# Smaller pieces for the last two weight groups of a streamed bilinear form

## The chip, the cores and the metric

The kernel runs on one core of a Trainium2 chip. The metric is the device time of one execution, in microseconds (us). The kernel before takes 88.63 us, the median of three runs (88.56 to 88.67). A profile is one recorded execution; its span, from the first to the last instruction, is 87.1 us in an execution that took 88.9 us. Times inside the profile are counted from the start of the span.

A core has several engines that run side by side: TensorE does matrix products (PE in the profile, with PEld for the loading of its stationary operand), VectorE is DVE, ScalarE is ACT, GpSimd is POOL and SyncE is SP. Data comes from the chip's memory through 16 DMA engines, which all transfers share.

## The reference

```python
batch, dim_i, dim_j, dim_k = 32, 256, 256, 128
# x: (32, 256), y: (32, 256), weight: (128, 256, 256), all float32
def reference(x, y, weight):
    return np.einsum('bi,bj,kij->bk', x, y, weight).astype(np.float32)
```

Every output element is x[b] · weight[k] · y[b]. The weight has 128 x 256 x 256 float32 values, which is 33.55 MB, and each is needed once. Reading it is the large part of the work.

## The kernel before

The 128 matrices weight[k] are treated in G = 32 groups of KK = 4. One group is laid out on 128 partitions, which hold 32 blocks of i for each of the 4 values of k, and within a partition there are IC = 8 rows of J = 256 values. A group is loaded by one DMA from the GpSimd queue, which turns float32 into bfloat16 on the way: 1 MB is read and 512 KB are written. The first group comes through another queue as float32.

```python
    w_v = weight.rearrange("(kk g) (ip ic) j -> g ip kk (ic j)", kk=KK, ic=IC)
    # ... x, y and group 0 are loaded ...
    def split(g):
        return [(0, 4), (4, 6), (6, 8)] if g == G - 1 else [(0, IC)]

    w_tiles = {}

    def load(g):
        for lo, hi in split(g):
            wt = wpool.tile([P, (hi - lo) * J], bf16, name=f"w{g}_{lo}")
            nc.gpsimd.dma_start(out=wt, in_=w_v[g][:, :, lo * J:hi * J])
            for ic in range(lo, hi):
                w_tiles[g, ic] = wt[:, (ic - lo) * J:(ic - lo + 1) * J]

    load(1)
    # ... an identity matrix is made ...
    for g in range(2, G):
        load(g)
    # ... xblk (x, one block per ic, masked per kk) and y4 are prepared ...
```

Every tile of the pool is a buffer of its own, so no load waits for a buffer. The loads share eight completion semaphores in turn, and for this reason a load is issued only when the load eight places before it has landed.

A group is then eight matmuls, one for each ic, that add up in one bank of PSUM, followed by one VectorE instruction that multiplies with y and sums over j:

```python
    for g in range(G):
        ps = pso.tile([P, J], f32)
        for ic in range(IC):
            nc.tensor.matmul(
                out=ps,
                lhsT=xblk[:, ic, :, :].rearrange("p b kk -> p (b kk)"),
                rhs=w_tiles[g, ic],
                start=(ic == 0), stop=(ic == IC - 1),
            )
        tmp = tmps.tile([P, J], f32)
        nc.vector.tensor_tensor_reduce(
            out=tmp, in0=ps, in1=y4, scale=1.0, scalar=0.0,
            op0=mult, op1=add, accum_out=acc[:, g:g + 1],
        )

    out_v = out.rearrange("b (kk g) -> b kk g", kk=KK)
    nc.sync.dma_start(out=out_v, in_=acc)
```

A matmul can start when the tile that holds its rows has landed as a whole. The last group (g = 31) comes in three pieces, of four, two and two rows; each other group comes in one piece.

Of the kernel before, what the change touches and what calls it, by code (L numbers as in the profile page):

```python
# [1 line left out]

# [4 lines left out]


@with_exitstack
def kernel(  # L10
    ctx: ExitStack,
    tc: tile.TileContext,
    x: bass.AP,
    y: bass.AP,
    weight: bass.AP,
    out: bass.AP,
):
    nc = tc.nc
    P = 128
    f32 = mybir.dt.float32  # L20
    bf16 = mybir.dt.bfloat16
    mult = mybir.AluOpType.mult
    add = mybir.AluOpType.add

    B, I = x.shape
    _, J = y.shape
    K, _, _ = weight.shape
    KK = P // B
    IP = P // KK
    IC = I // IP  # L30
    G = K // KK
    assert KK * B == P and IP * KK == P and IC * IP == I and G * KK == K

    consts = ctx.enter_context(tc.tile_pool(name="consts", bufs=1))
    wpool = ctx.enter_context(tc.tile_pool(name="wpool", bufs=1))
    psx = ctx.enter_context(tc.tile_pool(name="psx", bufs=1, space=bass.MemoryType.PSUM))
    pso = ctx.enter_context(tc.tile_pool(name="pso", bufs=4, space=bass.MemoryType.PSUM))
    tmps = ctx.enter_context(tc.tile_pool(name="tmps", bufs=2))


    w_v = weight.rearrange("(kk g) (ip ic) j -> g ip kk (ic j)", kk=KK, ic=IC)

    x_sb = consts.tile([B, I], f32)
    nc.scalar.dma_start(out=x_sb, in_=x)
    y_sb = consts.tile([B, J], f32)
    nc.scalar.dma_start(out=y_sb, in_=y)


    w0 = consts.tile([P, IC * J], f32)
    nc.sync.dma_start(out=w0, in_=w_v[0])  # L50

    def split(g):
        return [(0, 4), (4, 6), (6, 8)] if g == G - 1 else [(0, IC)]

    w_tiles = {}

# [9 lines that stand above are left out]
    ident = consts.tile([P, P], f32)  # L66
    nc.gpsimd.memset(ident, 0.0)  # L67
    nc.gpsimd.affine_select(  # L68
        out=ident, in_=ident, compare_op=mybir.AluOpType.not_equal, fill=1.0,
        base=0, pattern=[[-1, P]], channel_multiplier=1,  # L70
    )
    for g in range(2, G):
        load(g)

    mask = consts.tile([P, KK], f32)
    nc.vector.tensor_reduce(  # L76
        out=mask, in_=ident.rearrange("p (ip kk) -> p kk ip", kk=KK),
        axis=mybir.AxisListType.X, op=add,
    )


    x_rep = consts.tile([B, IC, IP, KK], f32)
    x_cols = x_sb.rearrange("b (ip ic) -> b ic ip", ic=IC)
    for ic in range(IC):
        nc.vector.tensor_copy(  # L85
            out=x_rep[:, ic, :, :],
            in_=x_cols[:, ic, :].unsqueeze(2).to_broadcast([B, IP, KK]),
        )
    xt_ps = psx.tile([P, IC, B], f32)
    for ic in range(IC):  # L90
        nc.tensor.transpose(  # L91
            out=xt_ps[:, ic, :],
            in_=x_rep[:, ic, :, :].rearrange("b ip kk -> b (ip kk)"),
            identity=ident[:B, :B],
        )


    xblk = consts.tile([P, IC, B, KK], bf16)
    for kk in range(KK):
        nc.vector.tensor_scalar(  # L100
            out=xblk[:, :, :, kk], in0=xt_ps, scalar1=mask[:, kk:kk + 1],
            scalar2=None, op0=mult,
        )


    JH = J // P
    yt_ps = psx.tile([P, JH, B], f32)
    for jh in range(JH):
        nc.tensor.transpose(  # L109
            out=yt_ps[:, jh, :], in_=y_sb[:, jh * P:(jh + 1) * P],  # L110
            identity=ident[:B, :B],
        )
    yt4 = consts.tile([P, JH, B, KK], f32)
    nc.vector.tensor_copy(  # L114
        out=yt4, in_=yt_ps.unsqueeze(3).to_broadcast([P, JH, B, KK])
    )
    y4_ps = psx.tile([P, J], f32)
    for jh in range(JH):
        nc.tensor.transpose(  # L119
            out=y4_ps[:, jh * P:(jh + 1) * P],  # L120
            in_=yt4[:, jh, :, :].rearrange("p b kk -> p (b kk)"),
            identity=ident,
        )
    y4 = consts.tile([P, J], f32)
    nc.vector.tensor_copy(out=y4, in_=y4_ps)  # L125

    w0b = wpool.tile([P, IC * J], bf16)
    for lo, hi in ((0, IC // 2), (IC // 2, IC)):
        nc.scalar.copy(out=w0b[:, lo * J:hi * J], in_=w0[:, lo * J:hi * J])  # L129
    for ic in range(IC):  # L130
        w_tiles[0, ic] = w0b[:, ic * J:(ic + 1) * J]

    acc = consts.tile([P, G], f32)
# [19 lines that stand above are left out]
# [1 line left out]
_INS = ['x', 'y', 'weight']  # L154
_OUTS = [((32, 128), 'float32')]


# [23 lines left out]
```

## Time and profile before

| What | Value |
|---|---|
| device time, median of three runs | 88.63 us (88.56 to 88.67) |
| span of the profiled execution | 87.1 us |
| TensorE busy / weight loads busy | 54.4 us (62%) / 32.6 us (37%) |
| VectorE, GpSimd, ScalarE busy | 18.6, 18.3 and 3.3 us |
| weight loads on the GpSimd queue | 33: 30 of 512 KB, 1 of 256 KB, 2 of 128 KB (as written) |
| read from memory over the span | 33.62 MB, 386 GB/s |

The busy shares say how long an engine worked over the whole span. They do not say what sets the end: for that one reads the chain of waits, which goes back from the last instruction to what released it, and the timeline of the last microseconds. In the view of the slices, the span is cut into 40 equal parts of about 2.18 us; a digit is a share in tenths.

### The profile page before, as it was taken

The page shows a single profiled execution, that of the slowest core. Times are in us where ns is not written, and L with a number is a line of the kernel's source. Part 1 is how long each engine was busy: PE and PEld are TensorE (multiplying, and loading weights), DVE is VectorE, ACT ScalarE, POOL GpSimd, SP SyncE. Part 2 cuts the span into 40 slices and gives each one's busy share as a digit, 9 for nine tenths or more (in the row PEclk, how much of TensorE's full clock was granted, in tenths as well). Part 3 has the DMA queues.
Part 4 walks back from the last instruction along what each step waited for, and adds up shares of the span by engine and source line. Part 5 has one row for each costly group of instructions (what it writes and reads, how often), then busy time and mean ns, then how long its engine had stood idle before and what let it go on. Part 6 is the DMA issues. An engine that isn't in the chain of part 4 may idle for free.

```text
span 87.1 us, 741 instructions
## 1 busy us (share of the span) xinstructions
PE 54.4 (62%) x268; PEld 32.6 (37%) x268; DVE 18.6 (21%) x79; ACT 3.3 (4%) x3; POOL 18.3 (21%) x39
## 2 busy tenths in 40 slices
PE   0416994667777843776487773754887544974870
PEld 0415653433343432433344432332444331543630
DVE  0893123011111120111101111111011211031030
ACT  2327000000000000000000000000000000000000
POOL 5980222222111221112222222012222200000000
PEclk9999999755555696557955598589555975569659
DMA  1899999999999999999999999999999999999700
GB/s 30 277 312 209 216 216 216 213 213 213 213 214 213 211 213 218 213 216 213 213 213 213 211 216 213 211 213 216 213 218 211 213 214 211 214 214 203 127 3 8
DMA packets 5139, 17.43 MB, mean 200 GB/s; under 512 B 720, under 2 KB 1040, under 8 KB 5008
## 3 DMA queue, kind: packets, MB, share of 16 engines
q0 software_dynamic: 4752, 16.26, 93.6%
q1 hardware_dynamic: 288, 1.07, 3.5%
q10 hardware_dynamic: 96, 0.07, 0.4%
q8 instruction: 2, 0.03, 0.1%
q14 instruction: 1, 0.01, 0.0%
HBM read 33.62 MB, written 0.02 MB: 386 GB/s over the span
## 4 chain that ended last, share of the span: by engine, by line
DMA 87%; PE 4%; POOL 3%; issue 2%; DVE 0%; POOLq 0%; DVEq 0%
DMA w<-in_weight_dram 87%; PE ps L137 4%; POOL w L60 3%; DVE tmp L144 0%; POOL ident L68 0%; POOL ident L67 0%; POOLq L68 0%; POOLq L165 0%; DVEq L176 0%
## 5 line engine op out<-in xcount | busy, mean ns | idle before, releaser
L137 PE MATMUL ps<-w,xblk 128*128 128x256 bf16 x248 | 50.8, 377 | 24.2 <-DMA w<-in_weight_dram 24.2
L137 PEld LDWEIGHTS <-xblk 128*128 128x128 bf16 x256 | 31.0, 130 | 46.9 <-DMA w<-in_weight_dram 34.3
L60 POOL DMA_DIRECT2D w<-in_weight_dram x33 | 17.7, 546 | 50.6 <-DMA w<-in_weight_dram 49.8
L144 DVE CUSTOM_DVE_ANT_0 tmp<-ps,y 128x256 f32<-128x256 f32 x32 | 13.6, 425 | 62.2 <-PE ps L137 62.2
L137 PE MATMUL ps<-w0b,xblk 128*128 128x256 bf16 x8 | 2.1, 411 | 1.6 <-ACT w0b L129 1.6
L91 PE MATMUL xt_ps<-ident,x_rep 32*128 32x32 f32 x8 | 1.1, 293 | 3.0 <-POOL ident L68 3.0
L144 DVE DVE_READ_ACCUMULATOR2_ANT acc<- 128x1 f32 x32 | 2.7, 83 | 0.0
L100 DVE TENSOR_SCALAR xblk<-xt_ps,mask 128x256 bf16<-128x256 f32 x4 | 2.5, 771 | 0.1
L129 ACT CAST w0b<-w 128x1024 bf16<-128x1024 f32 x2 | 2.0, 1042 | 3.2 <-DMA w<-in_weight_dram 3.2
L91 PEld LDWEIGHTS xt_ps<-ident,x_rep 32*128 32x128 f32 x8 | 0.9, 200 | 3.0 <-POOL ident L68 3.0
L85 DVE COPY x_rep<-x_sb 32x128 f32<-32x128 f32 x8 | 1.3, 236 | 2.4 <-DMA x_sb<-in_x_dram 2.4
L129 ACT ACT_TABLE_LOAD x1 | 1.3, 1283 | 1.6 <-PEq L165 1.6
L109 PE MATMUL yt_ps<-ident,y_sb 32*128 32x32 f32 x2 | 0.4, 300 | 1.1 <-DMA y_sb<-in_y_dram 1.1
L109 PEld LDWEIGHTS yt_ps<-ident,y_sb 32*128 32x128 f32 x2 | 0.3, 199 | 1.2 <-DMA y_sb<-in_y_dram 1.2
L125 DVE COPY y<-y_ps 128x256 f32<-128x256 f32 x1 | 0.4, 425 | 1.3 <-PE y_ps L119 1.3
L119 PE MATMUL y_ps<-ident,yt 128*128 128x128 f32 x2 | 0.6, 417 | 0.0
L119 PEld LDWEIGHTS y_ps<-ident,yt 128*128 128x128 f32 x2 | 0.4, 226 | 0.1
L114 DVE COPY yt<-yt_ps 128x256 f32<-128x256 f32 x1 | 0.4, 448 | 0.0
L76 DVE TENSOR_REDUCE mask<-ident 128x4 f32<-128x128 f32 x1 | 0.4, 369 | 0.0
L68 POOL TENSOR_SCALAR_AFFINE_SELECT ident<-ident 128x128 f32<-128x128 f32 x1 | 0.3, 322 | 0.1
L67 POOL MEMSET ident<- 128x128 f32 x1 | 0.2, 224 | 0.0
L165 POOL MEMSET const-float32-0.0<- 128x1 f32 x1 | 0.1, 99 | 0.2 <-issue 0.2
(3 smaller groups left out, 0.3 us busy)
## 6 DMA issues: line engine op xcount, KB each, us to landing
w<-in_weight_dram POOLq DMA_DIRECT2D x30, 512.0 KB, 19.4
w<-in_weight_dram SPq DMA_DIRECT2D x1, 1024.0 KB, 5.3
w<-in_weight_dram POOLq DMA_DIRECT2D x1, 256.0 KB, 18.3
w<-in_weight_dram POOLq DMA_DIRECT2D x2, 128.0 KB, 15.6
x_sb<-in_x_dram ACTq DMA_DIRECT2D x1, 32.0 KB, 1.7
y_sb<-in_y_dram ACTq DMA_DIRECT2D x1, 32.0 KB, 4.0
out_dram<-acc SPq DMA_DIRECT2D x1, 16.0 KB, 1.4
```

Of the source, the lines that this page charges most:

```text
L60: nc.gpsimd.dma_start(out=wt, in_=w_v[g][:, :, lo * J:hi * J])
L76: nc.vector.tensor_reduce(out=mask, in_=ident.rearrange("p (ip kk) -> p kk ip", kk=KK), axis=mybir.AxisListType.X, op=add,)
L85: nc.vector.tensor_copy(out=x_rep[:, ic, :, :], in_=x_cols[:, ic, :].unsqueeze(2).to_broadcast([B, IP, KK]),)
L91: nc.tensor.transpose(out=xt_ps[:, ic, :], in_=x_rep[:, ic, :, :].rearrange("b ip kk -> b (ip kk)"), identity=ident[:B, :B],)
L100: nc.vector.tensor_scalar(out=xblk[:, :, :, kk], in0=xt_ps, scalar1=mask[:, kk:kk + 1], scalar2=None, op0=mult,)
L109: nc.tensor.transpose(out=yt_ps[:, jh, :], in_=y_sb[:, jh * P:(jh + 1) * P], identity=ident[:B, :B],)
L114: nc.vector.tensor_copy(out=yt4, in_=yt_ps.unsqueeze(3).to_broadcast([P, JH, B, KK]))
L119: nc.tensor.transpose(out=y4_ps[:, jh * P:(jh + 1) * P], in_=yt4[:, jh, :, :].rearrange("p b kk -> p (b kk)"), identity=ident,)
L125: nc.vector.tensor_copy(out=y4, in_=y4_ps)
L129: nc.scalar.copy(out=w0b[:, lo * J:hi * J], in_=w0[:, lo * J:hi * J])
L137: nc.tensor.matmul(out=ps, lhsT=xblk[:, ic, :, :].rearrange("p b kk -> p (b kk)"), rhs=w_tiles[g, ic], start=(ic == 0), stop=(ic == IC - 1),)
L144: nc.vector.tensor_tensor_reduce(out=tmp, in0=ps, in1=y4, scale=1.0, scalar=0.0, op0=mult, op1=add, accum_out=acc[:, g:g + 1],)
```

## The change

The last group is loaded in four pieces instead of three: its last two rows come as two pieces of one row. The group before it (g = 30) is loaded in two pieces of four rows instead of one of eight. Nothing else is edited. The purpose is to let the last matmuls start before the whole of their group has landed, so that less work is left when the last byte arrives.

```diff
     def split(g):
-        return [(0, 4), (4, 6), (6, 8)] if g == G - 1 else [(0, IC)]
+        if g == G - 1:
+            return [(0, 4), (4, 6), (6, 7), (7, 8)]
+        if g == G - 2:
+            return [(0, 4), (4, 8)]
+        return [(0, IC)]
```

There are then 35 loads on the GpSimd queue instead of 33. The number and the order of the matmuls, of the weight loads of TensorE and of the VectorE instructions do not change. The first matmul of each new piece carries a wait for that piece.

## The prediction

> **What bounds the kernel now.** I read the page first, for the chain of waits and the slices, and then the end in detail: the chain in order of time, the timeline from 70 us, the DMA issues, and two tables by window. The chain and the slices:
>
> ```profile
> DMA 87%; PE 4%; POOL 3%; issue 2%; DVE 0%; POOLq 0%; DVEq 0%
> ...
> GB/s 30 277 312 209 216 216 216 213 213 213 213 214 213 211 213 218 213 216 213 213 213 213 211 216 213 211 213 216 213 218 211 213 214 211 214 214 203 127 3 8
> ...
> q8 instruction: 2, 0.03, 0.1%
> ```
>
> The stream of weights is the bound: 87% of the chain is its transfer, and the bytes written run at a flat 213 GB/s from slice 4 to slice 36. A group of 512 KB (524,288 bytes) takes 524,288 / 213,000 = 2.46 us. The change removes no byte, so all that it can save lies behind the stream. The last steps of the chain in order of time:
>
> ```profile
> 61.29 19.52 DMA w<-in_weight_dram
> 80.81 0.05 issue
> 80.85 3.44 PE ps L137 x16
> 84.30 0.02 issue
> 84.32 0.42 DVE tmp L144
> ```
>
> The last transfer on the chain is that of g = 30, not of g = 31: it lands at 80.81, and then sixteen matmuls, two whole groups, run in one unbroken row of 3.44 us. So TensorE, and not the last piece, sets the end. The timeline gives the pace of a group:
>
> ```profile
> 70.88 1.89 PE L137 MATMUL ps<-w,xblk 128*128 128x256 bf16 x8 [1.39 <-DMA w<-in_weight_dram]
> ...
> 78.43 1.05 PE L137 MATMUL ps<-w,xblk 128*128 128x256 bf16 x8 [0.60 <-DMA w<-in_weight_dram]
> ...
> 80.85 3.43 PE L137 MATMUL ps<-w,xblk 128*128 128x256 bf16 x16 [1.37 <-DMA w<-in_weight_dram]
> ```
>
> Eight matmuls take 1.89 us at one time and 1.05 us at another. The table by window shows why (columns: window, length, busy us and count of PE, PEld, DVE, ACT, POOL, granted clock, DMA share, GB/s). I cut it where the granted clock changes:
>
> ```profile
> 70.83:74.24 3.41, 2.03 (x9) 1.15 (x10) 0.43 (x2) 0.00 (x0) 0.00 (x0) 0.50 1.06 214
> 74.24:77.65 3.41, 3.40 (x16) 1.92 (x14) 0.43 (x2) 0.00 (x0) 0.00 (x0) 0.50 1.06 213
> 77.65:81.07 3.42, 1.45 (x12) 0.91 (x11) 0.87 (x4) 0.00 (x0) 0.00 (x0) 1.00 1.07 204
> 81.07:84.48 3.41, 3.21 (x16) 1.98 (x14) 0.59 (x3) 0.00 (x0) 0.00 (x0) 0.50 0.33 54
> ```
>
> A window with 1.45 us of TensorE work is followed by half clock, one with 3.40 us by full clock. The end falls into a half-clock window. One matmul took 0.42 us at half clock and 0.27 at full (the shortest and the longest in the view of the weight tiles). In a row they then follow each other every (1.89 - 0.42) / 7 = 0.21 us at half clock and every (1.05 - 0.27) / 7 = 0.11 us at full.
>
> When do the pieces of g = 31 land? The view of the DMA issues, asked for the windows that hold one issue each, gives the times from issue to landing:
>
> ```profile
> w<-in_weight_dram POOLq DMA_DIRECT2D x1, 256.0 KB, 18.3
> ...
> w<-in_weight_dram POOLq DMA_DIRECT2D x1, 128.0 KB, 16.5
> ...
> w<-in_weight_dram POOLq DMA_DIRECT2D x1, 128.0 KB, 14.7
> ```
>
> With the issue times 63.74, 66.24 and 68.68 of the timeline of POOL they land at 82.0, 82.7 and 83.4. The timeline of the last two microseconds has the eight matmuls of g = 31 start at 82.37, so its first piece waited some 0.35 us for TensorE. Its last matmul starts at 84.30 - 0.42 = 83.9, half a microsecond after the last landing. That is the slack that the change can reach.
>
> **What the Trainium skill says.** "TensorE: Matmul & The Clock Gate", section "Part 1: The HAM clock gate", has the clock either at half or at full, set by how busy the engine was in the last window of about 3.4 us, with windows that run free of the kernel. The trace agrees: windows of 3.41 us, only 0.50 and 1.00. "DMA: Bandwidth & Descriptors", section "Why a DMA increments its semaphore by 16 and not by 1", says that a transfer counts as landed only when the last of its 16 engines has posted. The trace agrees: the DMA share falls to 0.19 in the window from 82 to 83 us, so that about three engines of sixteen are left, and the final piece lands only after them. "Runtime: NRT & Kernel Launch", section "Instruction fetch mechanics", says that instructions are themselves fetched by DMA in blocks of 16 KiB; the page's q8 line has two such packets, 0.03 MB. They are an explanation for laggards that I cannot prove here. The same DMA page, section "Specifications", wants at least 512 B for line rate. The new one-row pieces write exactly 512 B per partition (256 values of 2 bytes); no transfer of this size is in this trace.
>
> **The change part by part.**
>
> The issues. The loads go from 33 to 35. POOL spends 0.55 us on each (17.7 us / 33), so 1.1 us more, beside an idle of 50.6 us. A load is issued when the one eight places before has landed. By the old times the fifth and fourth loads before the end now go at 63.74 and 66.24, the next at 68.68, and the last two when g = 26 and g = 27 land, about 70.9 and 74.1 by their matmuls. This is over 9 us before their bytes are due. It costs nothing on the path.
>
> The stream. Each DMA engine handles 8 of the 128 partitions, so it gets 8 more packets for g = 30 and 8 more for the last pieces, and two more completion packets. What does a packet cost beyond its bytes? From 20 to 30 us there are 586 packets of which 65 are completions, at 106.3% of 16 engines: 170 us / 521 = about 0.32 us for a packet of 4 KB. From 82.6 to 82.8 us five packets of 1 KB take 15.3%: 0.49 us / 5 = 0.098 us. The line through both has 0.023 us fixed per packet. But the share is over 100%, so packets overlap: by pace, 4 KB at 213 / 16 = 13.3 GB/s per engine is 0.308 us, and the bulk of the 1 KB packets (81.0 to 81.2 us) moved 210 GB/s, almost the same rate. So the cost by pace is about 0.002 us per packet. A completion takes 0.022 us (one packet, 0.7% of 16 engines, in 83.0 to 83.2 us). The sum is 16 x 0.002 + 2 x 0.022 = 0.08 us; if nothing overlapped, 16 x 0.023 + 0.044 = 0.41 us. I take 0.1: the last piece lands at 83.5.
>
> The work of g = 30. Its first half lands half a group earlier, at 80.81 - 1.23 = 79.6. Four matmuls at full clock take 0.6 us and are over by 80.2, when TensorE used to sit idle. The second half lands at 80.85; two matmuls at full clock and two at half end by 81.7. This frees TensorE about 0.7 us sooner than the 82.4 of before.
>
> The work of g = 31. TensorE now waits for its first piece, which lands at 82.05 and starts at 82.1. Eight matmuls in a row at half clock: the last starts at 82.1 + 7 x 0.21 = 83.57, if its piece is there. Piece (6, 7) is needed at 83.36 and should land near 83.15; piece (7, 8) lands at 83.5 and releases its matmul at 83.55. Both bounds meet. I put the last start at 83.65 and the end at 83.65 + 0.42 = 84.07, against 84.30: 0.23 us.
>
> What follows (0.42 us of VectorE, the output's DMA with 1.4 us to landing) does not change. The extra split of the last two rows alone would be worth little, as the piece of two rows was already 0.5 us early; the gain comes from splitting g = 30, which takes four matmuls out of the backlog. The sum: 88.63 - 0.23 = 88.4 us.
>
> **The rivals.**
>
> The stream pays more for small pieces than I take. With 0.41 us the last piece lands at 83.8, its matmul ends at 84.27 and the time is 88.6: no change. If a packet of 512 B cost the 0.098 us of one of 1 KB, the last pieces alone would add 8 x 0.098 = 0.78 us, and the time would be about 89.0. For it speaks that no such packet is in the trace; against it, that 1 KB packets ran at full rate.
>
> The clock. If the final window were at full clock, eight matmuls would be over soon after each landing in both kernels, and the last landing alone would set the end. The changed kernel would then end at 83.55 + 0.27 = 83.8 and take 88.15. The window before would need much more work for that: it gains about 0.6 us on 1.45, to 2.0, and 2.03 was followed by half clock from 70.83 on. I think it unlikely. That the three times lie within 0.11 us also speaks for one and the same state of the end.
>
> The laggards. Two or three DMA engines finish about 1 us after the rest. If what delays them (the instruction packets are one candidate) fell on the same engine, or on none, the end would move by some tenths either way in any kernel. Nothing in the change touches it.
>
> **Range and chances.** From 88.15 (full clock at the end) to 88.6 (dear packets), with a tenth for the spread of runs: 88.1 to 88.75. Two per cent are 1.8 us. To gain that the kernel would have to lose over half of the 3.5 us between the landing of g = 30 and the end, and the stream alone forbids it; to lose it, the small pieces would have to cost four times my worst sum. So the time stays within 2% with 0.98.
>
> **What the profile after would show.** The row of sixteen matmuls should be broken: four from 79.6, four from 80.9, eight from 82.1, with waits for DMA between. The last step of the chain before TensorE should be a piece of g = 31, with less than 2 us of matmuls behind it. The last landing should be at 83.4 to 83.6. I would be wrong if it came at 83.8 or later, if the final window had full clock, or if the span of DMA before 80.8 us changed.

## The result and the profile after

The changed kernel took 88.09 us (median of four runs, 88.00 to 88.16), against 88.59 us for four runs of the kernel before beside it. The ratio is 0.9944 with a 95% interval of 0.9926 to 0.9961. That is 0.5 us, about twice what was predicted, and 88.09 lies just under the predicted range. A longer measurement further down gives a smaller difference; most of this study is about the difference between the two.

The chain of waits of the changed kernel, first its shares from the page and then its last pieces in order of time (start, length, what):

```profile
DMA 90%; issue 5%; POOL 1%; DVE 0%; PE 0%; POOLq 0%; DVEq 0%
```

```profile
73.39 9.73 DMA w<-in_weight_dram
83.12 0.04 issue
83.17 0.28 PE ps L141
83.45 0.02 issue
83.47 0.42 DVE tmp L148
```

TensorE's share of the chain went from 4% to less than half a per cent. The last transfer on the chain is now the last piece of g = 31, which lands at 83.12, and one matmul of 0.28 us stands behind it. Before, the last transfer on the chain was g = 30's, with sixteen matmuls behind it. The timeline of TensorE at the end, and the granted clock by window (columns as in the prediction's table; 1.00 is TensorE's full clock, 0.50 half of it):

```profile
78.09 3.60 PE L141 MATMUL ps<-w,xblk 128*128 128x256 bf16 x16 [0.55 <-DMA w<-in_weight_dram]
...
81.88 1.56 PE L141 MATMUL ps<-w,xblk 128*128 128x256 bf16 x8 [0.19 <-DMA w<-in_weight_dram]
```

```profile
78.79:82.20 3.41, 3.22 (x16) 2.00 (x15) 0.87 (x4) 0.00 (x0) 0.00 (x0) 0.50 1.02 169
82.20:85.61 3.41, 1.16 (x8) 0.50 (x6) 0.43 (x2) 0.00 (x0) 0.00 (x0) 1.00 0.06 9
```

The sixteen matmuls are g = 29 and both halves of g = 30, done at half clock before g = 31 begins to land. The eight of g = 31 start at 81.88, and from 82.20 on they run at full clock. They take 1.56 us, where eight in a row at half clock took 1.89. Two things are thus new at the end: the order of the work and the clock. The order was predicted only in part: TensorE does wait for the first piece of g = 31, but the four and four matmuls of g = 30 with waits between them are not there, because g = 29 and g = 30 run as one row at half clock. The full clock at the end had been named beforehand as a sign of being wrong. And a third thing differs: the matmuls of g = 29 start at 78.09 here and at 78.43 before, so the stream itself was 0.34 us earlier, although nothing ahead of g = 30 was changed.

### The profile page after: what moved, and what is told of

Its sections match the earlier page's. It is cut to its first block, busy times and chain, and to the rows that moved or that the text cites. A ratio compares the mean times of both kernels' runs of the same rounds, so it can differ in the third digit from the quotient of the medians.

```text
span 86.2 us, 743 instructions
## 1 busy us (share of the span) xinstructions
PE 53.4 (62%) x268; PEld 32.1 (37%) x268; DVE 18.6 (22%) x79; ACT 3.3 (4%) x3; POOL 19.4 (22%) x41
## 4 chain that ended last, share of the span: by engine, by line
DMA 90%; issue 5%; POOL 1%; DVE 0%; PE 0%; POOLq 0%; DVEq 0%
DMA w<-in_weight_dram 90%; POOL w L64 1%; DVE tmp L148 0%; PE ps L141 0%; POOL ident L71 0%; POOLq L180 0%; POOLq L169 0%; DVEq L180 0%
## 5 line engine op out<-in xcount | busy, mean ns | idle before, releaser
L141 PE MATMUL ps<-w,xblk 128*128 128x256 bf16 x248 | 49.9, 370 | 24.6 <-DMA w<-in_weight_dram 24.5
L141 PEld LDWEIGHTS <-xblk 128*128 128x128 bf16 x256 | 30.4, 128 | 46.7 <-DMA w<-in_weight_dram 33.9
L64 POOL DMA_DIRECT2D w<-in_weight_dram x35 | 18.7, 542 | 54.2 <-DMA w<-in_weight_dram 53.4
```

Source lines behind the costliest of these rows:

```text
L141: nc.tensor.matmul(out=ps, lhsT=xblk[:, ic, :, :].rearrange("p b kk -> p (b kk)"), rhs=w_tiles[g, ic], start=(ic == 0), stop=(ic == IC - 1),)
```

## Experiments

**Theory A**: the backlog of TensorE behind the landing of g = 30 sets the end, but only where the last window has half clock; the windows run free of the kernel, so both ends occur among the runs of one kernel, and the change removes the late one. **Theory B**: the first profile of before merely had a late stream. **Theory C**, on the tail of the stream itself: the last piece waits for two DMA engines that were held up by instruction packets, that is, by the transfers that bring the engines their program.

### The two kernels again, and each half of the change alone

`again_before` and `again_after` are the two kernels unchanged. The other two are one part each:

```diff
 only_g30_split
-            return [(0, 4), (4, 6), (6, 7), (7, 8)]
+            return [(0, 4), (4, 6), (6, 8)]
 only_g31_split
-        if g == G - 2:
-            return [(0, 4), (4, 8)]
```

> The kernel before, unchanged, for a second profile and the spread of its spans. Theory A (TensorE's backlog sets the end, and the clock in the last window varies from run to run): the last weight piece lands within 0.1 us of a fixed distance from the landing of g = 29 (5.0 us), sixteen matmuls in a row follow the landing of g = 30, and the end of the matmuls lies 0.4 us (full clock) to 0.9 us (half clock) behind the last landing. Theory B (the first profile merely had a late stream, by 0.3 us at its start): the first load of g = 1 lands near 8.3 us instead of 8.60, and the span falls by the same 0.3 us to about 86.8.

> The changed kernel, unchanged. Theory A: the last piece lands 5.1 us after g = 29, the matmuls end 0.3 us (full clock) to 0.5 us (half clock) behind it, time 88.0 to 88.2. Theory B: the early stream of its first profile (8.34 us for g = 1) does not come back, and the time rises to 88.3 or 88.4, the 0.23 us that were predicted.

> Only g = 30 in two halves; g = 31 as before in four, two and two rows. Theory A: nearly the whole gain, since the four matmuls taken from the backlog are here: 88.1 to 88.2, the last landing about 0.05 us earlier than with the one-row pieces and two matmuls behind it. Rival (the one-row pieces carry the gain): 88.5 to 88.6.

> Only the last two rows of g = 31 in two pieces of one; g = 30 whole as before. Theory A: no gain, 88.5 to 88.7, sixteen matmuls in a row behind the landing of g = 30, and no wait for the last two pieces. Rival (the one-row pieces carry the gain): 88.1 to 88.2.

All four were timed on one chip beside 58 runs of the kernel before. The ratio is the time of a kernel over that of the kernel before, with its 95% interval. The kernel's own copy has 0.9996 (0.9974 to 1.0017): the same. A further run of before, of 89.32 us, lies more than 1.5% above the fastest and is left out.

| Kernel | Runs | Mean | Median | Lowest to highest | Runs of 88.5 us or more | Ratio to before (95%) |
|---|---|---|---|---|---|---|
| before, with its copy | 80 | 88.34 | 88.27 | 87.72 to 88.99 | 29 | |
| after, again | 22 | 88.11 | 88.11 | 87.71 to 88.45 | 0 | 0.9972 (0.9952 to 0.9992) |
| only g = 30 split | 14 | 88.14 | 88.16 | 87.94 to 88.31 | 0 | 0.9986 (0.9964 to 1.0009) |
| only g = 31 split | 14 | 88.23 | 88.10 | 87.85 to 88.88 | 3 | 0.9989 (0.9960 to 1.0018) |

The kernel before is not a kernel of 88.6 us. Its runs spread over 1.3 us, and more than a third of them are at 88.5 or above. The changed kernel has the same shortest runs and none of the long ones. The means differ by 0.24 us. The first four runs of before (88.46 to 88.67) lie in the upper part of this spread. The interval of only g = 30 split still holds 1, and that of only g = 31 split does too; what separates them is the upper end, 88.31 against 88.88. The splitting of g = 30 alone came out as expected (88.1 to 88.2). For the splitting of g = 31 alone 88.5 to 88.7 was expected, and that missed: its median is 88.10, and only its three long runs lie there.

The second profile of before shows the other end. Its timeline of TensorE, and its windows:

```profile
80.62 1.05 PE L137 MATMUL ps<-w,xblk 128*128 128x256 bf16 x8 [0.73 <-DMA w<-in_weight_dram]
81.87 1.08 PE L137 MATMUL ps<-w,xblk 128*128 128x256 bf16 x6 [0.20 <-DMA w<-in_weight_dram]
83.21 0.38 PE L137 MATMUL ps<-w,xblk 128*128 128x256 bf16 x2 [0.26 <-DMA w<-in_weight_dram]
```

```profile
76.16:79.57 3.41, 2.86 (x14) 1.76 (x13) 0.51 (x4) 0.00 (x0) 0.00 (x0) 0.50 1.06 209
79.57:82.99 3.42, 2.36 (x17) 1.34 (x16) 0.87 (x4) 0.00 (x0) 0.00 (x0) 1.00 0.72 123
```

This is the same kernel as in the first profile, but the last windows have full clock. g = 30 takes 1.05 us and is done before g = 31 begins, there is no backlog, and the matmuls end at 83.59 instead of 84.28. The row of sixteen behind the landing of g = 30, which Theory A had expected here too, is not there; the end 0.4 us behind the last landing (83.17), its number for full clock, is. Half of Theory B holds as well: the ninth load, which waits for the first to land, was issued at 8.62 here and at 8.88 in the first profile. But the changed kernel, too, was issued late the second time (8.90) and still took 88.13 in that run. A stream that starts 0.3 us later is part of the spread of both kernels, not of the change.

The record of the single runs ties the two ends to the clock without any edit. Each run lists its mean granted clock, and the values fall into groups. In the profiled run with half clock at the end it was 0.726, in the one with full clock 0.743.

| Mean granted clock of a run of before | Runs of the 80 | Mean time | Lowest to highest | Runs of 88.5 us or more |
|---|---|---|---|---|
| 0.705, 0.706, 0.725 or 0.726 | 21 | 88.71 | 88.51 to 88.99 | 21 |
| 0.715 to 0.723, or 0.735 to 0.743 | 43 | 88.15 | 87.72 to 88.58 | 2 |

The other 16 runs lie between and around these groups, with times of both kinds. The grouping was made after the fact, but the 74 runs of before on the chip of the next experiment repeat it: 19 runs in the first group, 88.50 to 88.94, and 38 in the second, one of them at 88.5 or more. The two groups interleave, so it is not simply that a longer run has a lower mean, and a late stream alone would not sort the times in this way.

### The clock held at half, and held at full

To hold the clock at half, most of the work ahead of g = 30 is narrowed to 16 columns (the output then lacks these products):

```diff
+            n = 16 if 24 <= g <= 29 and ic > 0 else J
             nc.tensor.matmul(
-                out=ps,
+                out=ps[:, 0:n],
                 lhsT=xblk[:, ic, :, :].rearrange("p b kk -> p (b kk)"),
-                rhs=w_tiles[g, ic],
+                rhs=w_tiles[g, ic][:, 0:n],
```

To hold the clock at full, TensorE gets extra work whose result nobody reads:

```diff
+        for _ in range(extra(g)):   # 3 for g = 16 to 18, 6 for g = 19 to 29
+            nc.tensor.matmul(
+                out=idle, lhsT=xblk[:, 0, :, :].rearrange("p b kk -> p (b kk)"),
+                rhs=w_whole[g][:, 0:2 * J], start=True, stop=True,
+            )
```

> The kernel before with seven of the eight matmuls of g = 24 to 29 narrowed from 256 to 16 columns: same instructions and loads, so little TensorE work before g = 30 that its last windows should be at half clock in every run. Theory A (backlog at half clock): sixteen matmuls in an unbroken row behind the landing of g = 30, 3.6 us, the matmuls end 0.9 to 1.1 us behind the last landing, times 88.5 to 88.9 with no fast end. Rival (the spread of the times comes from the stream, not from the clock): same spread as before, 87.8 to 88.9.

> The same narrowing in the changed kernel. Theory A: the wait for the first piece of g = 31 stays in place, eight matmuls at half clock behind it, and the end comes 0.35 us sooner than in the narrowed kernel before: 88.2 to 88.5. Rival: no difference between the two beyond 0.1 us.

> The kernel before with extra matmuls (512 columns, into a PSUM bank that nobody reads) behind the groups 16 to 29, three each and then six, so that TensorE is busy over four fifths of the time and should stay at full clock to the end. Theory A: g = 30 is done before the first piece of g = 31 lands, the matmuls end 0.4 us behind the last landing, times 87.9 to 88.2: the slow ends are gone without any smaller piece. Rival (stream): spread and median as before, 88.3.

> The same extra matmuls in the changed kernel. Theory A: nothing is left for the smaller pieces to gain at full clock: one matmul less behind the last landing (0.1 us) against 0.07 us of stream, so within 0.1 us of the kernel before with the same extra matmuls. Rival (the pieces gain by themselves, whatever the clock): 0.2 us or more faster than it.

All four ran on one chip; the kernel before beside them had a median of 88.30 us.

| Clock at the end | before: mean, median (range) | after: mean, median (range) | Difference of the means |
|---|---|---|---|
| half | 88.80, 88.74 (88.43 to 89.42), 21 runs | 88.41, 88.40 (88.19 to 88.61), 22 runs | 0.39 |
| full | 88.16, 88.19 (87.90 to 88.37), 22 runs | 88.07, 88.08 (87.82 to 88.39), 22 runs | 0.09 |

The last full windows of the profiles show the clock that was meant: at half the narrowed kernel before and then after, at full the kernel before with extra matmuls. For the runs without a profile only the times speak.

```profile
81.45:84.87 3.42, 3.06 (x15) 1.83 (x13) 0.76 (x3) 0.00 (x0) 0.00 (x0) 0.50 0.15 24
```

```profile
80.25:83.67 3.42, 2.94 (x13) 1.42 (x11) 0.43 (x2) 0.00 (x0) 0.00 (x0) 0.50 0.61 90
```

```profile
76.98:80.39 3.41, 3.33 (x20) 1.59 (x18) 0.76 (x4) 0.00 (x0) 0.00 (x0) 1.00 1.05 204
80.39:83.81 3.42, 2.58 (x17) 1.40 (x16) 0.61 (x3) 0.00 (x0) 0.00 (x0) 1.00 0.46 76
```

The ends of the two chains at half clock, before and then after:

```profile
80.87 0.05 issue
80.92 3.61 PE ps L138 x16
84.52 0.02 issue
```

```profile
81.91 0.04 issue
81.95 1.88 PE ps L142 x8
83.83 0.02 issue
```

And at full clock, before and then after:

```profile
83.17 0.04 issue
83.22 0.39 PE ps L145 x2
83.61 0.02 issue
```

```profile
83.27 0.04 issue
83.31 0.28 PE ps L149
83.59 0.02 issue
```

At half clock the kernel before has sixteen matmuls behind the landing of g = 30 and the changed one eight behind the first piece of g = 31, and the difference is 0.39 us by the means, 0.34 by the medians. At full clock both chains end with the last landing, two matmuls against one. The one-row piece saves 0.11 us there, but it landed 0.10 us later in these two profiles, so their ends lie 0.02 us apart; by the means of all runs the change brings 0.09. With the clock held at full, the kernel before has no run above 88.37: its long ends are gone without any change of the pieces. The 95% interval of the difference of means, from runs drawn again at random, is 0.28 to 0.50 at half clock and 0.00 to 0.18 at full. The two intervals lie apart: the clock decides what the change is worth, as Theory A has it. The means of the kernel before with the clock held, 88.80 and 88.16, are also close to those of its two groups of runs above, 88.71 and 88.15.

### What the tail of the stream waits for

The changed kernel, with seven of eight matmuls of g = 1 to 29 left out (the output lacks them), so that TensorE's program is short:

```diff
-        for ic in range(IC):
+        n = 1 if 1 <= g <= 29 else IC
+        for ic in range(n):
 ...
-                start=(ic == 0), stop=(ic == IC - 1),
+                start=(ic == 0), stop=(ic == n - 1),
```

> The changed kernel with seven of the eight matmuls of each of g = 1 to 29 left out, so that TensorE's program is about a fifth as long; all loads stay. Theory C (the two instruction packets of 16 KB each hold one DMA engine for about 0.9 us, and the last piece waits for these two engines): the two packets are gone from the queue that carries instructions, the last landing comes 0.7 to 0.8 us sooner after the start of the stream, at 82.3 to 82.5, and the time is 87.5 to 87.7, against 88.4 of the kernel with narrowed matmuls that ends at half clock too. Rival (the late engines are late by nature): last landing at 83.1 or later and 88.3 to 88.4.

It took 87.58 us (8 runs), ratio 0.9918 (0.9889 to 0.9948), where the narrowed changed kernel had 1.0010 (0.9994 to 1.0026), each against the kernel before on its own chip. Some queues of the short program, and under them those of the changed kernel (packets, MB, share of 16 engines):

```profile
q10 hardware_dynamic: 96, 0.07, 0.3%
q14 instruction: 1, 0.01, 0.0%
```

```profile
q10 hardware_dynamic: 96, 0.07, 0.3%
q8 instruction: 2, 0.03, 0.1%
q14 instruction: 1, 0.01, 0.0%
```

The two instruction packets of q8 are gone. The end of the chain in the short program:

```profile
81.15 0.05 issue
81.20 1.90 PE ps L142 x8
83.10 0.02 issue
```

The first piece of g = 31 lands at 81.15, against 81.91 in the narrowed kernel: 0.76 us sooner, with all loads in place. The last piece, issued at 72.76 and 9.7 us under way, lands at 82.5, as Theory C has it. In the window from 82 to 83 us the share of the DMA engines is 0.02, where the changed kernel still has 0.14, which is about two engines of sixteen.

The traces also show when the delay comes in, and that is not at the end. From 8.7 to 31 us the narrowed kernel and the short program issue their loads at the same times within 0.02 us, although TensorE does much more in the first of them. Then they part, first the narrowed kernel and under it the short program:

```profile
30.77 0.53 POOL L64 DMA_DIRECT2D w<-in_weight_dram  x1 [1.91 <-DMA w<-in_weight_dram]
34.53 0.53 POOL L64 DMA_DIRECT2D w<-in_weight_dram  x1 [3.23 <-DMA w<-in_weight_dram]
```

```profile
30.79 0.53 POOL L64 DMA_DIRECT2D w<-in_weight_dram  x1 [1.91 <-DMA w<-in_weight_dram]
33.21 0.53 POOL L64 DMA_DIRECT2D w<-in_weight_dram  x1 [1.89 <-DMA w<-in_weight_dram]
```

Between the two issues, from 32 to 33 us, the narrowed kernel has the first of its instruction packets:

```profile
q8 instruction: 1, 0.02, 5.6%
```

That is 0.9 us of one engine. The landing that POOL waits for comes 1.3 us later than in the short program, and the landings after it stay late to the end. The second packet runs near 72 us in both the narrowed and the changed kernel. Theory C has its numbers, and the rival has not. A less busy TensorE alone does not explain it: up to 31 us it made no difference, and the narrowed kernels, which left TensorE idle for the last groups, kept both packets and landed late. That the eight matmuls take 1.90 us shows that the short program ended at half clock, like the narrowed one; its granted clock is not in the trace.

### More pieces, and fewer

```diff
 finer_pieces
         if g == G - 1:
-            return [(0, 4), (4, 6), (6, 7), (7, 8)]
+            return [(0, 2), (2, 4), (4, 6), (6, 7), (7, 8)]
         if g == G - 2:
-            return [(0, 4), (4, 8)]
+            return [(0, 2), (2, 4), (4, 6), (6, 8)]
 halves_only
         if g == G - 1:
-            return [(0, 4), (4, 6), (6, 7), (7, 8)]
+            return [(0, 4), (4, 8)]
 early_halves
-        if g == G - 2:
+        if g == G - 2 or 5 <= g <= 7:
             return [(0, 4), (4, 8)]
```

> g = 30 in four pieces of two rows and g = 31 in two, two, two, one and one. Theory A: TensorE already idles before the first piece of g = 31 in the changed kernel, so finer pieces ahead of the last one take nothing from behind the last landing except at half clock, where eight matmuls can start 0.6 us earlier and the last piece alone is left: at most 0.1 us sooner, paid for with about 0.1 us of stream. 88.0 to 88.2, the same as the changed kernel. Rival (the more pieces the better): 87.9 or less.

> g = 30 and g = 31 both in two halves only. Theory A: four matmuls are left behind the last landing, 0.6 us at full and 1.05 us at half clock, against 0.3 to 0.5 in the changed kernel, and 0.05 us less stream: 88.3 to 88.6. Rival (only the split of g = 30 matters): 88.1 to 88.2.

> The changed kernel with g = 5, 6 and 7 in two halves as well: 38 loads, as many as the finer pieces, but the three added ones early. In the finer pieces the time lies 2.05 us above the span, in all other kernels 1.79. If the number of loads makes this, it is 2.05 here too and the time is 88.3 to 88.4; if it is that the last loads are issued only 5 us before the end, it stays 1.79 and the time is 88.1 to 88.2.

Halves only took 88.26 us (14 runs, ratio 1.0001, 0.9979 to 1.0024). In its profile four matmuls, 0.61 us, stand behind the last landing at 83.09. It has two runs above 88.5. The time lies between what Theory A (88.3 to 88.6) and the rival (88.1 to 88.2) expected. The profile shows the backlog moved behind the last landing, and the gain against the kernel before is no longer seen; the interval still overlaps that of the changed kernel, so the loss itself is not clear of the noise.

The finer pieces took 88.48 us (22 runs, ratio 1.0007, 0.9985 to 1.0030), which neither side expected. The end of its chain has the same shape as the changed kernel's, with its last landing at 83.30:

```profile
78.98 4.32 DMA w<-in_weight_dram
83.30 0.04 issue
83.34 0.28 PE ps L141
```

Its span is 86.47 us in the mean of its runs, 0.15 more than the changed kernel's 86.32. And its time is 2.05 us above its span, that of the changed kernel 1.78; so a quarter of a microsecond lies outside of what the profile records. The early halves were to tell whether this comes with the number of loads (38 in both, 35 in the changed kernel) or with loads that are issued late. There too the time is 2.06 us above the span, so it goes with the number of loads or of packets. What it is, the profile cannot show. The early halves took 89.22 us in all (6 runs, ratio 1.0088, 1.0053 to 1.0123), above both expected times, because their span is longer as well. The slices of their stream:

```profile
GB/s 30 301 294 210 217 212 206 153 209 210 217 212 217 212 219 210 213 215 212 212 213 215 213 213 212 217 212 210 215 213 215 210 213 221 210 203 210 154 8 8
```

One slice, from 15.3 to 17.5 us, falls to 153 GB/s; about 0.6 us of stream is lost there (60 of 213, of 2.19 us), when the first halves are on their way (g = 4 lands at 16.1, the first half of g = 5 at 18.1). Its cause was not tried further and stays open.

## Why the prediction was right or wrong

**The bound and the mechanism** were right: the row of sixteen behind the landing of g = 30 is gone, TensorE waits for the first piece of g = 31, and the last transfer of the chain is a piece of g = 31. The course of g = 30 was not: I had its first four matmuls at full clock and over by 80.2, and in the first profile after they run at half clock in one row with g = 29, from 78.09 to 81.7. It cost nothing there, because the first piece of g = 31 lands later still.

**The issues** cost nothing: the last one is at 73.39, when its bytes are over 9 us away.

**The stream** was to pay 0.1 us for the small packets. From the start of g = 29's matmuls to the last landing it is 83.12 - 78.09 = 5.03 us after and 83.4 - 78.43 = 4.97 before, 0.06 us more. The rival of dear 512-byte packets fell.

**The one-row pieces** were to be worth little. At full clock they are worth one matmul of 0.11 us, and alone they left the long ends in place.

**What failed is the step on the clock**, which put the final window at half clock and held full clock there for unlikely. It failed in two places. First: "That the three times lie within 0.11 us also speaks for one and the same state of the end." It did not: the kernel before has two ends, and 80 runs spread over 1.3 us with a mean of 88.34. The profile that I reckoned from (88.9 us, stream 0.3 us late, half clock at the end) was one of its longest runs. I took a difference that holds for this end from a median of 88.63, and so the absolute time came out 0.3 us too high: 88.4 against 88.09 and 88.11. Second: the rival of full clock at the end, at 88.15, was put aside as unlikely, and it is what the first profile after shows in its last eight matmuls. I had asked whether one window, from 77.65 to 81.07, would gain enough work. In the profile after the window before the end runs from 78.79 to 82.20 and holds 3.22 us of work; I had not reckoned that with windows that run free the answer differs from run to run.

**The size.** At half clock I predicted 0.23 us; with the clock held there it is 0.39. The term that was too small is the backlog of before: 3.45 us from 80.85 to 84.30 in my profile, where the first two matmuls still had full clock, and 3.60 when all sixteen have half. The changed kernel's side was right: 3.22 us from the second half of g = 30 to the end by my sum, and in the narrowed kernel 83.83 - 80.68 = 3.15. For full clock I had written that the last landing alone sets the end of both kernels, and there the difference is 0.09. Over the mixture of both ends 0.24 us was measured, which agrees with the 0.23 by a cancelling of the two and not by a correct reckoning. The first comparison's 0.50 is above both: its four runs of before were all long ones, which 33 of the 80 later runs are (88.46 or more). Why all four were is not shown.

**The laggards** were left open in the prediction, with the instruction packets as a candidate. The short program and the times of the issues make them the cause of 0.76 us. The kernels before and after have the same two packets.

## What to carry to other kernels

When a stream sets the time, look at what stands between the last landing and the end: a smaller last piece only helps if the engine behind it has no backlog from the group before. Here the split of the group before the last removed the long runs by itself (none in 14), and finer pieces than that brought no further gain that is clear of the noise. Where TensorE has only half its time to do and its clock alternates, one profile shows one of several ends; get the spread of the runs and their mean clock, and test the change with the clock held low and held high, before a gain below 1% is believed. More pieces are not free even where the stream hardly slows: 38 loads instead of 35 cost 0.26 us outside of the span.

## What the runs showed of the hardware

The granted clock at the end is a matter of chance for a kernel that keeps TensorE busy for 62% of its span: of the same kernel, one profile had half clock from 81.07 and another full clock from 79.57. The Trainium skill, "TensorE: Matmul & The Clock Gate", section "Part 1: The HAM clock gate", says that the windows do not start with the kernel and that the count of slow matmuls varies from run to run. The runs agree: the edges of the last windows lay at 77.65 and 81.07 in one profile of the kernel before and at 76.16 and 79.57 in the other. The times of before spread by 1.3 us, and by 0.47 us with the clock held full, so much of the spread went with the clock. Not all of it: with the clock held at half, the kernel before still spread from 88.43 to 89.42. With 3.33 us of work in a window of 3.41 the clock stayed full to the end (1.00 in both last windows of the kernel with extra matmuls), and the mean clock of that run was 0.842, against 0.726 and 0.743 in the two profiles of before. Extra matmuls that compute nothing made the kernel before faster (0.9976, 0.9956 to 0.9996).

A program of TensorE that is long enough to be fetched while it runs holds back single DMA engines: without the two 16 KB instruction packets the last pieces landed 0.76 us sooner, and the kernel was at 87.58 us. The Trainium skill, "Runtime: NRT & Kernel Launch", section "Instruction fetch mechanics", calls the cost of such a fetch mostly hidden; here, where the DMA engines are the bound, a packet of 0.9 us on one engine made every landing behind it late. This was seen with work left out; whether a kernel that does all the work can have so short a program was not tried.
